# Attention gates as 48 extra columns behind the query projection's token tiles

## The chip, the cores and the metric

The kernel runs on one core of a Trainium2 chip. The metric is the device time of one execution in microseconds, a median of several runs. The engines are named as in the profile: PE is TensorE (matmuls), PEld its loads of the stationary operand, DVE is VectorE, ACT is ScalarE, POOL is GpSimd, SP is SyncE, which only issues transfers.

## The reference, cut to what matters

The program is a decoder trunk of two layers for 512 tokens of width 1024 in float32. Layer 0 has a gated convolution as its mixer, layer 1 a sparse attention with three branches (compressed, selected, windowed); each mixer stands between two half-step SwiGLU networks. The change touches one thing in the attention: the gates that weigh the three branches of the 16 heads.

```python
q, kc, vc, ks, vs, kw, vw, gl = jnp.split(h @ w_in, offs, axis=-1)
gates = jax.nn.sigmoid(gl.astype(f32)).reshape(bsz, seq, G, Hg, 3).transpose(0, 2, 3, 1, 4)
...
out = gb[..., 0:1] * o_c + gb[..., 1:2] * o_s + gb[..., 2:3] * o_w
```

`gl` are the last 48 columns of the attention's input projection (16 heads x 3 branches); `h` is the normalized input, 512 x 1024. For each token, head and branch one number in 0 to 1 results.

## The kernel before, in words

**Precision.** A float32 product is made of three fp32r matmuls: each operand is split into a high part and a low remainder (`split`, lines 175 to 177: ACT copies the high part, DVE subtracts), and the products high-high, high-low and low-high are summed in PSUM (`mm3`, lines 184 to 187). A matmul has a stationary operand, loaded first (PEld), and a moving operand, whose columns stream past it. In the profile a matmul is written out<-moving,stationary.

**Activations** lie transposed: `h` is 8 tiles of 128 features x 512 tokens, each with a high and a low part (`h[0][k]`, `h[1][k]`; hhi and hlo in the profile).

**Two kinds of projection.** `project` (line 204) holds a weight tile of 128 x 128 and streams 512 tokens past it; its result has features on the partitions. `natural` (line 737) holds a tile of 128 tokens x 128 features of `h` and streams 256 columns of weights past it; its result has tokens on the partitions, which queries, keys and values need. `natural(c, each)` loads its weights at once, in two parts of 4 x 128 rows (`nsa_in`, line 711), and returns two jobs, each for half of the tokens: a PSUM tile `nat`, two token tiles, 8 steps of k each, three matmuls a step, so 48 matmuls; then `each` takes the result out of PSUM.

**The gates** (line 946) use `project`: the 48 columns, padded to 128 with zeros, are the stationary operand, so that 24 matmuls of 512 columns give 48 x 512 in PSUM (`gl`). ACT takes the exponential of the negative, four transposes on TensorE turn it to tokens on partitions (`pg`), DVE adds 1 and takes the reciprocal into `gsb`. The attention reads `gsb` (lines 1048 and 1103).

**Where this stands.** `nsa` (line 715) first makes four projections with `head_start` (`hs`), then the preparation in `es2` (lines 829 to 862): the compressor of keys and values in steps (`c0`, `c1`; its copies `t` out of `hs`, its split blocks `flh` and `fll`, its matmuls `ph`), the query projection of group 0 (`q0`, projection 0), the key projections 8 and 6, the gates, and the value projection 7. Then `attend` runs 32 units, with the remaining projections spread among them in steps.

**Buffers and order.** Weights come through a shared pool of three buffers each for the raw, high and low part (`wraw`, `whi`, `wlo`; line 189); a weight is transferred by SP's queue as soon as a raw buffer is free and split as soon as its other two are. Projections 8, 6 and 7 take their second part from a pool of their own (`nw`). PSUM has eight banks: two for each of the tags nat, s, t and o; a tile named mm takes the first three in turn (`six`, line 75). The program is written without an explicit order among engines: the tile framework puts each engine's instructions in order when the program is built, by a planner that simulates when each is ready and otherwise prefers the one earlier in the program, and sets the semaphores. Each engine then runs its list in order.

## Time and profile before

| | |
|---|---|
| median of 3 runs | 1948.66 us (1947.72 to 1952.35) |
| the profiled execution's own time | 1950.15 us |
| its span, first to last instruction | 1948.4 us |
| granted TensorE clock | 1.00 |
| PE busy / DVE busy / ACT busy | 98% / 75% / 45% |
| head_start of the attention ends, query projection begins | 1280.0 us |
| gates' projection | 1327.5 to 1333.0 us |
| gates' transposes | 1341.2 to 1341.5 us |

How to read it: an instruction has a start and a duration from the span's start; a matmul's duration includes a latency that overlaps the next matmul, so the pace of a stream is read from the starts. Groups show busy time, the mean of one, and the idle time of the engine ahead of them with what ended it. A row of a stretch shows its length and then the busy time of PE, PEld, DVE, ACT and POOL with the number of instructions, the granted clock, the share of the DMA engines and GB/s.

### The profile page before, as it was taken

The numbers are of one execution on the slowest core, as the hardware profiler recorded it, in microseconds if no ns is written. First come the engines' busy times: TensorE is split into PE (matmuls) and PEld (weight loads), VectorE is DVE, ScalarE is ACT, GpSimd is POOL, SyncE is SP. The second block draws the span as 40 slices with busy tenths as digits, with TensorE's granted clock in tenths as the row PEclk, the third lists the DMA queues.
The fourth block names the chain that finished last, engine by engine and source line by source line (L and its number), as shares of the span: only waits on it lengthen the run. The fifth ranks groups of instructions, "written<-read, shape, count | busy, mean of one in ns | idle before, by whom it ended". The sixth has DMA issues, their size and how long they took to land.

```text
span 1948.4 us, 32290 instructions
## 1 busy us (share of the span) xinstructions
PE 1905.9 (98%) x12600; PEld 1727.0 (89%) x12600; DVE 1458.0 (75%) x2519; ACT 869.3 (45%) x1401; POOL 194.4 (10%) x294
## 2 busy tenths in 40 slices
PE   6999999999999999999999999999999899999999
PEld 4888888898899898999989899999888789898989
DVE  7888888674467586868868686885787987685965
ACT  4322222342235353434635343465887865353532
POOL 0000000100010000000000000002444420000000
PEclk9999999999999999999999999999999999999999
DMA  8889889522145664634566463235433433665621
GB/s 313 310 318 329 311 323 326 202 98 98 65 122 160 158 173 125 168 104 120 154 165 174 125 167 103 78 127 144 112 69 66 115 82 115 186 163 143 174 82 65
DMA packets 113670, 313.42 MB, mean 161 GB/s; under 512 B 13995, under 2 KB 14267, under 8 KB 113516
## 3 DMA queue, kind: packets, MB, share of 16 engines
q1 hardware_dynamic: 96208, 273.88, 41.4%
q0 software_dynamic: 17216, 37.33, 11.1%
q8 instruction: 99, 1.62, 0.3%
q14 instruction: 55, 0.45, 0.1%
q10 hardware_dynamic: 92, 0.14, 0.0%
HBM read 308.15 MB, written 3.15 MB: 160 GB/s over the span
## 4 chain that ended last, share of the span: by engine, by line
PE 86%; DVE 5%; ACT 4%; DMA 2%; issue 2%; SPq 1%; POOL 0%; DVEq 0%; ACTq 0%; POOLq 0%
PE gu L186 13%; PE gu L185 13%; PE gu L187 13%; PE y L186 7%; PE y L185 7%; PE y L187 7%; PE hs L186 2%; PE hs L187 2%; PE hs L185 2%; PE cv L186 2%; PE cv L185 2%; PE cv L187 2%; PE ty L186 2%; PE ty L185 2%; PE ty L187 2%
## 5 line engine op out<-in xcount | busy, mean ns | idle before, releaser
L176 ACT ACTIVATE whi<-wraw 128x1024 fp32r<-128x1024 f32 (+2 forms) x274 | 270.8, 996 | 494.5 <-PE y L186 203.8
L177 DVE TENSOR_TENSOR wlo<-wraw,whi 128x1024 fp32r<-128x1024 f32 (+2 forms) x274 | 311.3, 1141 | 59.4 <-ACT whi L176 57.4
L186 PE MATMUL gu<-hlo,whi 128*128 128x256 f32 (+1 forms) x880 | 278.2, 316 | 0.0
L185 PE MATMUL gu<-hhi,whi 128*128 128x256 f32 (+1 forms) x880 | 278.1, 316 | 0.0
L187 PE MATMUL gu<-hhi,wlo 128*128 128x256 f32 (+1 forms) x880 | 277.4, 315 | 0.0
L186 PE MATMUL y<-alo,whi 128*128 128x512 f32 x587 | 229.2, 390 | 0.2 <-DVE alo L177 0.2
L185 PE MATMUL y<-ahi,whi 128*128 128x512 f32 x587 | 229.1, 390 | 0.0
L187 PE MATMUL y<-ahi,wlo 128*128 128x512 f32 x587 | 228.9, 390 | 0.0
L131 DVE CUSTOM_DVE_ANT_0 adaraw<-adaraw,cond 128x1024 f32<-128x1024 f32 x144 | 174.5, 1222 | 41.8 <-DMA adaraw<-in_adaw 39.2
L185 PEld LDWEIGHTS gu<-hhi,whi 128*128 128x128 f32 x880 | 165.2, 188 | 12.9
L187 PEld LDWEIGHTS gu<-hhi,wlo 128*128 128x128 f32 x880 | 165.2, 188 | 12.3
L186 PEld LDWEIGHTS gu<-hlo,whi 128*128 128x128 f32 x880 | 165.2, 188 | 12.0
L523 POOL DMA_DIRECT2D qa<-in_ffi x54 | 65.0, 1204 | 794.5 <-DMA qa<-in_ffi 261.8
L185 PEld LDWEIGHTS y<-ahi,whi 128*128 128x128 f32 x587 | 110.2, 188 | 23.6 <-ACT ahi L176 0.4
L186 PEld LDWEIGHTS y<-alo,whi 128*128 128x128 f32 x587 | 110.2, 188 | 23.6 <-DVE alo L177 0.5
L187 PEld LDWEIGHTS y<-ahi,wlo 128*128 128x128 f32 x587 | 110.2, 188 | 23.3
L599 DVE SCALAR_TENSOR_TENSOR x<-y,mods,x 128x512 f32<-128x512 f32 x72 | 53.4, 750 | 93.7 <-PE y L187 93.6
L185 PE MATMUL gu<-th,qbh 128*128 128x256 f32 x432 | 119.6, 277 | 2.2 <-ACT qbh L176 2.2
L187 PE MATMUL gu<-th,qbl 128*128 128x256 f32 x432 | 119.6, 277 | 0.7 <-DVE qbl L177 0.7
L186 PE MATMUL gu<-tl,qbh 128*128 128x256 f32 x432 | 119.3, 276 | 0.0
L185 PE MATMUL gu<-th,qah 128*128 128x256 f32 x432 | 119.2, 276 | 0.0
L186 PE MATMUL gu<-tl,qah 128*128 128x256 f32 x432 | 119.2, 276 | 0.0
(314 smaller groups left out, 5059.9 us busy)
## 6 DMA issues: line engine op xcount, KB each, us to landing
adaraw<-in_adaw SPq DMA_DIRECT2D x144, 512.0 KB, 6.2
wraw<-in_ffi SPq DMA_DIRECT2D x122, 512.0 KB, 4.1
qa<-in_ffi SPq DMA_DIRECT2D x108, 256.0 KB, 4.0
qa<-in_ffi POOLq DMA_DIRECT2D x54, 512.0 KB, 6.8
wraw<-in_ffo SPq DMA_DIRECT2D x72, 384.0 KB, 4.2
a<-in_ffi SPq DMA_DIRECT2D x54, 256.0 KB, 4.1
wraw<-in_cwi SPq DMA_DIRECT2D x24, 512.0 KB, 3.3
wraw<-in_nwi SPq DMA_DIRECT2D x20, 512.0 KB, 3.9
```

The source lines that it names most:

```text
L131: nc.vector.tensor_tensor_reduce(out=raw, in0=raw, in1=cond, scale=1.0, scalar=0.0, op0=ALU.mult, op1=ALU.add, accum_out=m)
L176: nc.scalar.activation(hi, src, AF.Copy)
L177: nc.vector.tensor_tensor(lo, src, hi, ALU.subtract)
L185: nc.tensor.matmul(o, sh, mh, start=first, stop=False)
L186: nc.tensor.matmul(o, sh, ml, start=False, stop=False)
L187: nc.tensor.matmul(o, sl, mh, start=False, stop=last)
L523: nc.gpsimd.dma_start(qa, bass.AP(tensor=a21.tensor, offset=a21.offset, ap=[a21.ap[0], [0, 2], a21.ap[1]]), accum_op=ALU.add)
L599: lambda d, o: nc.vector.scalar_tensor_tensor(x[d], o, mod(s, 2, d), x[d], op0=ALU.mult, op1=ALU.add))
```

## The change

The gates lose their own projection. The query projection of group 0 gets a second PSUM tile (`gl`) and the gate weights as a third weight tile. In each step of k, while it goes through the token tiles, it streams the first 48 columns of the gate weights' high and low part past the same token tile as the query weights: two matmuls of 48 columns ahead of the two with hhi, one ahead of the one with hlo. The result has tokens on the partitions at once, 4 x 48 columns in one PSUM bank; the four transposes go, and Exp, addition and reciprocal follow at the end of the query projection's second half, on 128 partitions x 192 columns. The gate weights are allocated, transferred and split together with the query projection's. Without a gate, the matmuls of `natural` and their order are those of before.

```diff
-            def natural(c, each, own=None):
+            def natural(c, each, own=None, gate=None):
                 w = nsa_in(c, own)
+                if gate:
+                    gw, go = weights(nwg, KD, P), psum("gl")
...
                         for k in range(KD):
-                            wh, wl = w[k // 4]
-                            mm3(oc, h[0][k][:, tk], h[1][k][:, tk], wh[:, k % 4, :], wl[:, k % 4, :],
-                                k == 0, k == KD - 1)
+                            wh, wl = [p[:, k % 4, :] for p in w[k // 4]]
+                            hh, hl = [p[k][:, tk] for p in h]
+                            first, last = k == 0, k == KD - 1
+                            if gate:
+                                gc = slice((2 * hf + t) * 48, (2 * hf + t + 1) * 48)
+                                gh, gl = [p[:, k, 0:48] for p in gw]
+                                nc.tensor.matmul(go[:, gc], hh, gh, start=first, stop=False)
+                                nc.tensor.matmul(go[:, gc], hh, gl, start=False, stop=False)
+                            nc.tensor.matmul(oc, hh, wh, start=first, stop=False)
+                            nc.tensor.matmul(oc, hh, wl, start=False, stop=False)
+                            if gate:
+                                nc.tensor.matmul(go[:, gc], hl, gh, start=False, stop=last)
+                            nc.tensor.matmul(oc, hl, wh, start=False, stop=last)
                     each(hf, o)
+                    if gate and hf:
+                        gate(go)
...
-                q0 = natural(0, raw(query_tiles(0), vq))
+                q0 = natural(0, raw(query_tiles(0), vq), gate=partial(gates, gsb))
...
-                g = gates(es2, h, gsb)
-                next(g)
...
-                next(g, None)
...
-    def gates(es, h, gsb):
-            o = psum("gl")
-            w = weights(nwg, KD, P)
-            project(o, w, 0, h, [(k, k) for k in range(KD)], True, True)
-            e = tmp("gle")[0:48]
-            nc.scalar.activation(e, o[0:48], AF.Exp, scale=-1.0)
-            yield
-            pg = psum("pg", "o")
-            for t in range(NB):
-                nc.tensor.transpose(pg[:, t * 48:(t + 1) * 48], e[:, t * P:(t + 1) * P], ident[0:48, 0:48])
-            ge = tmp("ge", NB * 48)
-            nc.vector.tensor_scalar(ge, pg[:, 0:NB * 48], 1.0, None, op0=ALU.add)
-            nc.vector.reciprocal(gsb.rearrange("p a b -> p (a b)"), ge)
+    def gates(gsb, o):
+        n = NB * 48
+        e = tmp("gle", n)
+        nc.scalar.activation(e, o[:, 0:n], AF.Exp, scale=-1.0)
+        nc.vector.tensor_scalar(e, e, 1.0, None, op0=ALU.add)
+        nc.vector.reciprocal(gsb.rearrange("p a b -> p (a b)"), e)
```

## The prediction

> **What bounds the kernel now.** I read the page's totals first, then the chain of waits.

> ```profile
> span 1948.4 us, 32290 instructions
> PE 1905.9 (98%) x12600; PEld 1727.0 (89%) x12600; DVE 1458.0 (75%) x2519; ACT 869.3 (45%) x1401; POOL 194.4 (10%) x294
> ...
> PE 86%; DVE 5%; ACT 4%; DMA 2%; issue 2%; SPq 1%; POOL 0%; DVEq 0%; ACTq 0%; POOLq 0%
> ```

> TensorE is busy 98% of the span, and 86% of the chain that ended last is its matmuls. The average says nothing about the stage that is edited, so next I read the busy time by stretches of the attention layer's preparation and of the attention behind it (length, then busy time of each engine).

> ```profile
> 1280.00:1291.30 11.30, 11.30 (x98) 11.30 (x97) 10.82 (x13) 8.66 (x12) 0.00 (x0) 1.00 0.52 174
> 1291.30:1303.00 11.70, 11.70 (x103) 11.70 (x102) 9.55 (x19) 5.42 (x9) 0.00 (x0) 1.00 0.38 128
> 1303.00:1315.00 12.00, 11.59 (x98) 11.15 (x97) 11.83 (x23) 9.08 (x12) 0.00 (x0) 1.00 0.50 156
> 1315.00:1327.40 12.40, 12.28 (x104) 12.04 (x103) 11.83 (x30) 5.87 (x10) 0.00 (x0) 1.00 0.36 115
> 1327.40:1333.00 5.60, 5.60 (x27) 4.58 (x26) 5.16 (x13) 3.49 (x4) 0.79 (x1) 1.00 0.71 220
> 1333.00:1345.00 12.00, 12.00 (x104) 11.74 (x103) 5.44 (x11) 7.07 (x11) 2.18 (x4) 1.00 0.86 201
> ...
> 1363.00:1400.00 37.00, 34.50 (x252) 30.64 (x251) 27.34 (x90) 30.17 (x77) 18.14 (x36) 1.00 0.54 133
> 1400.00:1600.00 200.00, 186.89 (x1263) 164.58 (x1262) 169.50 (x471) 156.87 (x378) 83.24 (x167) 1.00 0.36 83
> ```

> From 1280 to 1345 us TensorE stands still for 0.41 + 0.12 us in all, at a granted clock of 1.00. DVE is its near rival only from 1303 to 1327 (11.83 of 12.00). So whatever TensorE is given or spared here goes almost whole into the time. In the attention, from 1363 us on, it idles 2.50 + 13.11 us.

> **What is removed.** The gates' own projection and its four transposes, in order of time, each with the first instruction behind it:

> ```profile
> 1327.52 0.39 PE L185 MATMUL gl<-hhi,whi 128*128 128x512 f32 x1
> ...
> 1333.02 0.27 PE L938 MATMUL pk<-ident,kd 128*128 128x128 f32 x1
> ...
> 1341.15 0.44 PE L955 MATMUL pg<-ident,gle 48*128 48x48 f32 x4
> 1341.53 0.39 PE L185 MATMUL nat<-whi,hhi 128*128 128x256 f32 x1
> ```

> The 24 matmuls of 512 columns take 1333.02 - 1327.52 = 5.50 us (229 ns each; the 0.39 is a latency that overlaps the next one). The transposes take 1341.53 - 1341.15 = 0.38 us. Nothing else could have run on TensorE in either place. Removed: 5.88 us.

> **What is added.** The query projection of group 0 gets 4 token tiles x 8 k x 3 = 96 matmuls of 48 moving columns. Their stationary operand is the token tile, 128x128, which a neighbouring projection matmul uses too. Does the second use of a tile load it again? In the kernel before, the first two matmuls of each triple already share it (hhi), and the groups of loads say:

> ```profile
> L185 PEld LDWEIGHTS nat<-whi,hhi 128*128 128x128 f32 x256 | 48.4, 189 | 0.6 <-ACT kq L1029 0.5
> L186 PEld LDWEIGHTS nat<-wlo,hhi 128*128 128x128 f32 x256 | 48.3, 189 | 0.3 <-DVE wlo L177 0.3
> ```

> 256 loads for each: every matmul loads its own stationary operand, shared or not. So the edit adds 96 loads of 128 columns, and the question is their pace behind matmuls too short to hide them. The trace has such places: four matmuls of 1 column (L271), and an fp32r matmul of 128 columns in the attention (loads in order of time):

> ```profile
> 1259.00 0.53 PEld L271 LDWEIGHTS pr<-ones,nacc 128*128 128x128 f32 x4
> 1259.44 0.19 PEld L187 LDWEIGHTS hs<-hhi,wlo 128*128 128x128 f32 x1
> ...
> 1394.53 0.19 PEld L1133 LDWEIGHTS o<-ptl,vn 128*128 128x128 f32 x1
> 1394.64 0.66 PEld L1076 LDWEIGHTS s<-k,q 128*128 128x128 f32 x4
> ```

> (1259.44 - 1259.00) / 4 = 110 ns, and 1394.64 - 1394.53 = 110 ns again. For comparison the pace of the 256-column matmuls of this projection, 48 of them in its first half, and the slowest stream of columns in the trace:

> ```profile
> 1280.02 0.28 PE L185 MATMUL nat<-whi,hhi 128*128 128x256 f32 x1
> ...
> 1285.68 0.28 PE L185 MATMUL nat<-whi,hhi 128*128 128x256 f32 x1
> ...
> 4.40 7.16 PE L699 MATMUL pt<-oh,rbn 33*128 33x512 f32 x8 [4.40 <-DMA oh<-in_onehot]
> ```

> That is 5.66 / 48 = 118 ns for 256 columns, so 0.46 ns a column and 22 ns for 48. Even at the plain f32 rate of L699, 7.16 / 8 / 512 = 1.75 ns a column, 48 columns take 84 ns, less than the load. The load sets the price however the columns stream. Bounds for one added matmul: 22 ns below (if the shared load fell away) and 118 ns above (the pace of its neighbours); I take 112, close to the 110 of the load rows. 96 x 0.112 = 10.8 us, bounds 2.1 and 11.3.

> [...]

> **What is moved.** The gate weights' transfer, their split, the Exp with its table load, and the addition and reciprocal:

> ```profile
> 1250.61 3.44 SPq L196 DMA_DIRECT2D wraw<-in_nwi  x2
> ...
> 1278.49 1.32 ACT L888 ACTIVATE t<-hs 64x256 f32<-64x256 f32 x2 [0.69 <-DVE t L886]
> 1279.60 1.07 ACT L176 ACTIVATE whi<-wraw 128x1024 fp32r<-128x1024 f32 x1
> ...
> 1280.70 1.23 DVE L177 TENSOR_TENSOR wlo<-wraw,whi 128x1024 fp32r<-128x1024 f32 x1 [0.23 <-ACT whi L176]
> ...
> 1334.12 1.28 ACT L951 ACT_TABLE_LOAD   x1
> 1335.41 0.59 ACT L951 ACTIVATE gle<-gl 48x512 f32<-48x512 f32 x1
> ...
> 1341.71 0.34 DVE L957 TENSOR_SCALAR ge<-pg 128x192 f32<-128x192 f32 x1
> 1342.09 1.35 DVE L958 RECIPROCAL gsb<-ge 128x192 f32<-128x192 f32 x1
> ```

> The order of allocation makes the gate weights third in the shared ring of three weight buffers, in the place that keys' projection 8 has now: its transfer is the second of the two issued by 1254 us on SP's queue, long before its use, and its split is the ACT and DVE pair at 1279.60 and 1280.70. The gate's low half is needed by the second matmul of the query projection, at 1280.14. If the split stays where that pair is, it ends at 1281.93 and TensorE waits 1.8 us. But ACT was idle 0.69 us ahead of 1278.49, and the split now stands ahead of the copies `t` in the program, so it can begin near 1278.2, when the first weights' buffer comes free, and end near 1280.6. I take 0.6 us, bounds 0 and 1.8. Queued behind it are the copies `t` on ACT and DVE, which only the compressor waits for; the projection's longer stay (11.3 + 10.8 us) hides them.

> Projection 8 then has to take the first buffer that the query projection gives back, 12 of its matmuls and 12 gate matmuls before its end (12 x 0.118 + 12 x 0.112 = 2.8 us), and its split takes 1.07 + 1.23 = 2.3 us. It just fits while ACT and DVE are free: 0.2 us, bounds 0 and 1.8 (one operation of 1.2 us ahead of it on each engine). Exp, table load, addition and reciprocal, 3.6 us in two engines, fall into a stretch with ACT busy 5.42 of 11.70 and DVE 9.55; nothing reads the gates before the attention: 0. If that cover were gone they would cost their 3.6 us. Against this, DVE gets the longer query projection to run ahead in, and the 0.53 us of TensorE's stalls up to 1327 may go: -0.3, bounds -0.5 and 0.

> **The sum.** -5.9 + 10.8 + 0.6 + 0.2 - 0.3 = +5.4 us. The profiled execution took 1950.15 us (span 1948.4 and 1.75 around it), so 1955.6 by its own measure; it lies 1.5 us above the median, 1948.66, and against that the forecast is 1954.1 us, 0.28% slower.

> **The rivals.** The first ends on the other side: *the shared tile is held*, and an added matmul costs only its stream. Then 96 x 22 ns = 2.1 us, minus 5.9: -3.8, 1944.9 us. It decides from a mean price under 5.88 / 96 = 61 ns. For it speaks only that two neighbours share the tile; against it the 256 loads of the second matmul of a triple. Chance 0.05.

> *The gate weights come late*: both waits at their upper bound, 10.8 - 5.9 + 1.8 + 1.8 = +8.5, 1957.2 us. For it speaks that all three buffers are held to the query projection's end, against it that ACT and DVE have little else there. Chance 0.16.

> *The removed projection was a cover.* Behind it runs projection 7, whose weights came just in time:

> ```profile
> 1328.65 1.06 ACT L176 ACTIVATE whi<-wraw 128x1024 fp32r<-128x1024 f32 x1 [2.80 <-DMA wraw<-in_nwi]
> ...
> 1329.75 1.23 DVE L177 TENSOR_TENSOR wlo<-wraw,whi 128x1024 fp32r<-128x1024 f32 x1
> ```

> They end at 1330.98; with 5.5 us less ahead of it the projection would want them near 1328.1 and wait 2.9 us: +8.3, 1957.0 us. Against it: the gate weights leave the ring of transfers and buffers at the same place, so each later weight moves up by one. Chance 0.06.

> *The attention's order turns out otherwise.* Its instructions are put in order by a planner from their simulated readiness, and buffers rotate one step differently. TensorE idles 15.6 us there; a third of it, 5.2 us, gained or lost, gives 1948.9 or 1959.3 us. Nothing in the profile speaks for a sign: 0.14 for a gain (0.05 of it large enough to pass below the bound), 0.07 for a loss.

> **How the numbers follow.** A measurement of this kernel tells about 0.3% (5.8 us) from no change, so from 1942.8 to 1954.5 it is the same. The forecast has 0.52: with its small terms from 0 to 1 us, 0.37 of it lies within the bound and 0.15 above. Slower by over 0.3%: 0.15 + 0.16 + 0.06 + 0.07 = 0.44. Within: 0.37 + 0.05 + 0.09 = 0.51. Faster: 0.05. The range of 8 in 10 runs from 1947, which leaves out the held tile and a large gain, to 1959, which takes in both late weights and their bound on the load's pace.

> **What would show it.** Right: 96 more loads on TensorE in the query projection, its two halves lasting 11.3 + 10.8 us, added matmuls 110 to 118 ns apart, no gl matmuls of 512 columns, one table load still between the first and the last. Wrong: loads fewer than matmuls or a pace under 61 ns (the held tile); over 1 us of TensorE's idle at the query projection's first matmuls or at projection 8's, released by a low half (late weights); a wait at projection 7 (the cover); TensorE's idle from the attention's start to its end more than 3 us from 15.6.

## The result, and the profile after

The changed kernel takes 1956.53 us, the median of 18 runs (1953.89 to 1979.27); the kernel before takes 1949.11 us, also over 18 runs (1946.53 to 1952.35). The ratio is 1.0051, with a 95% interval of 1.0036 to 1.0066: slower, and by more than the 0.28% of the forecast, whose size of 5.4 us against the new 1949.11 would have been 1954.5 us. The medians lie 7.4 us or 0.38% apart; the means, 1958.96 and 1949.05 us, have the ratio 1.0051, because two of the 18 runs lie far above the others (1972.49 and 1979.27). The profiled execution took 1960.1 us. First its page (totals, then the line of the chain of waits that gives shares by engine):

```profile
span 1958.3 us, 32424 instructions
PE 1913.9 (98%) x12668; PEld 1736.5 (89%) x12668; DVE 1458.8 (74%) x2519; ACT 869.6 (44%) x1401; POOL 193.9 (10%) x294
...
PE 86%; DVE 6%; ACT 4%; DMA 2%; issue 2%; SPq 0%; POOL 0%; DVEq 0%; ACTq 0%; POOLq 0%
```

There are 12668 - 12600 = 68 matmuls more, and as many loads: 96 came, 24 + 4 went, and none of the 96 shares the load of its neighbour. Next the busy time of the kernel after by stretches, from the last of the head start to the end of the attention's own matmuls (length, then PE, PEld, DVE, ACT, POOL, the granted clock, the transfers). The borders are here the first matmuls of each part: query projection, projection 8, compressor's matmuls mixed with projection 6, projection 7 and the turning of keys and queries, attention.

```profile
1281.17:1304.23 23.06, 22.41 (x195) 22.21 (x194) 14.38 (x16) 10.56 (x14) 0.00 (x0) 1.00 0.30 104
1304.23:1315.54 11.31, 11.31 (x98) 11.31 (x97) 7.82 (x18) 5.36 (x8) 0.00 (x0) 1.00 0.47 141
1315.54:1340.58 25.04, 24.62 (x205) 23.91 (x203) 24.30 (x53) 15.92 (x22) 0.00 (x0) 1.00 0.41 135
1340.58:1364.92 24.34, 24.34 (x213) 24.23 (x212) 9.90 (x24) 11.88 (x21) 7.92 (x17) 1.00 0.73 170
1364.92:1586.70 221.78, 206.21 (x1375) 179.43 (x1373) 184.84 (x532) 184.53 (x450) 101.05 (x203) 1.00 0.38 89
```

The query projection lasts 23.06 us instead of 11.28 (1280.02 to 1291.30 before): +11.78. From its first matmul to the first attention logit (1364.92) it is 83.75 us; the same stretch of before is 78.24 us. So the edited stage costs +5.5 us. The attention took 221.78 us against 221.94. The rows of the kernel before for its last two parts, beside the last two above:

```profile
1333.02:1358.27 25.25, 25.25 (x217) 25.01 (x216) 7.78 (x15) 12.33 (x20) 7.09 (x17) 1.00 0.63 140
1358.27:1580.21 221.94, 206.36 (x1375) 179.39 (x1373) 185.12 (x532) 184.32 (x450) 100.91 (x203) 1.00 0.38 88
```

Where the extra matmuls stand is seen in the order of time on PE, with the idle time in brackets:

```profile
1281.17 0.29 PE L754 MATMUL gl<-whi,hhi 128*128 128x48 f32 x1
...
1281.50 0.28 PE L757 MATMUL nat<-wlo,hhi 128*128 128x256 f32 x1
1282.42 0.29 PE L755 MATMUL gl<-wlo,hhi 128*128 128x48 f32 x1 [0.65 <-DVE wlo L177]
...
1282.87 0.19 PE L754 MATMUL gl<-whi,hhi 128*128 128x48 f32 x1
...
1283.56 0.19 PE L754 MATMUL gl<-whi,hhi 128*128 128x48 f32 x1
...
1340.46 0.28 PE L187 MATMUL ph<-whi,fll 128*128 128x256 f32 x1
1340.58 0.27 PE L949 MATMUL pk<-ident,kd 128*128 128x128 f32 x1
```

One step of k, with three narrow and three wide matmuls, lasts 1283.56 - 1282.87 = 0.69 us; three wide ones lasted 0.354, so a narrow one costs 0.112 us. The first matmul with the gate weights' low half waits for it, although the planner has put two wide matmuls ahead of it. And the last two rows show the other side of the change: the compressor's last matmul is followed at once by the transpose that before stood behind the 24 matmuls of the gates.

The remaining difference of this profile lies outside the edited stage. Of the 9.9 us by which the two spans differ, 1.2 lie ahead of the stage, 5.5 in it, -0.2 in the attention and 3.4 behind it. The mean clock is 0.997: in two places, from 629.1 for 3.4 us and from 1612.2 for 6.8 us, TensorE ran at half its clock. Together that is 10.2 us at half clock, worth at most 5.1 us. The kernel before has the second place too, in another execution of it (below).

### The profile page after: what moved, and what is told of

Same layout as the page of the kernel before. It is cut to its first block, busy times and chain, and to the rows that moved or that the text cites. A ratio compares the mean times of both kernels' runs of the same rounds, so it can differ in the third digit from the quotient of the medians.

```text
span 1958.3 us, 32424 instructions
## 1 busy us (share of the span) xinstructions
PE 1913.9 (98%) x12668; PEld 1736.5 (89%) x12668; DVE 1458.8 (74%) x2519; ACT 869.6 (44%) x1401; POOL 193.9 (10%) x294
## 4 chain that ended last, share of the span: by engine, by line
PE 86%; DVE 6%; ACT 4%; DMA 2%; issue 2%; SPq 0%; POOL 0%; DVEq 0%; ACTq 0%; POOLq 0%
PE gu L186 13%; PE gu L187 13%; PE gu L185 13%; PE y L186 7%; PE y L185 7%; PE y L187 7%; PE hs L186 2%; PE hs L187 2%; PE hs L185 2%; PE cv L186 2%; PE cv L185 2%; PE cv L187 2%; PE ty L186 2%; PE ty L185 2%; PE ty L187 2%
## 5 line engine op out<-in xcount | busy, mean ns | idle before, releaser
L176 ACT ACTIVATE whi<-wraw 128x1024 fp32r<-128x1024 f32 (+2 forms) x274 | 271.2, 997 | 500.5 <-PE y L186 213.7
L177 DVE TENSOR_TENSOR wlo<-wraw,whi 128x1024 fp32r<-128x1024 f32 (+2 forms) x274 | 312.9, 1147 | 66.7 <-ACT whi L176 64.8
L186 PE MATMUL gu<-hlo,whi 128*128 128x256 f32 (+1 forms) x880 | 278.2, 316 | 0.0
L185 PE MATMUL gu<-hhi,whi 128*128 128x256 f32 (+1 forms) x880 | 278.0, 316 | 0.0
L187 PE MATMUL gu<-hhi,wlo 128*128 128x256 f32 (+1 forms) x880 | 277.4, 315 | 0.0
L186 PE MATMUL y<-alo,whi 128*128 128x512 f32 x587 | 229.2, 390 | 0.1
L185 PE MATMUL y<-ahi,whi 128*128 128x512 f32 x587 | 229.0, 390 | 0.0
L187 PE MATMUL y<-ahi,wlo 128*128 128x512 f32 x587 | 228.9, 390 | 0.0
L185 PEld LDWEIGHTS gu<-hhi,whi 128*128 128x128 f32 x880 | 165.2, 188 | 12.9
L187 PEld LDWEIGHTS gu<-hhi,wlo 128*128 128x128 f32 x880 | 165.2, 188 | 12.3
L186 PEld LDWEIGHTS gu<-hlo,whi 128*128 128x128 f32 x880 | 165.2, 188 | 12.0
L186 PEld LDWEIGHTS y<-alo,whi 128*128 128x128 f32 x587 | 110.2, 188 | 23.5 <-DVE alo L177 0.5
L187 PEld LDWEIGHTS y<-ahi,wlo 128*128 128x128 f32 x587 | 110.2, 188 | 23.4
L185 PEld LDWEIGHTS y<-ahi,whi 128*128 128x128 f32 x587 | 110.2, 188 | 23.2
L185 PE MATMUL gu<-th,qbh 128*128 128x256 f32 x432 | 120.3, 278 | 2.4 <-ACT qbh L176 2.4
L187 PE MATMUL gu<-th,qbl 128*128 128x256 f32 x432 | 120.3, 279 | 0.7 <-DVE qbl L177 0.7
L186 PE MATMUL gu<-tl,qbh 128*128 128x256 f32 x432 | 120.1, 278 | 0.0
L185 PE MATMUL gu<-th,qah 128*128 128x256 f32 x432 | 119.2, 276 | 0.0
L186 PE MATMUL gu<-tl,qah 128*128 128x256 f32 x432 | 119.2, 276 | 0.0
```

What stands on the lines that cost most here:

```text
L176: nc.scalar.activation(hi, src, AF.Copy)
L177: nc.vector.tensor_tensor(lo, src, hi, ALU.subtract)
L185: nc.tensor.matmul(o, sh, mh, start=first, stop=False)
L186: nc.tensor.matmul(o, sh, ml, start=False, stop=False)
L187: nc.tensor.matmul(o, sl, mh, start=False, stop=last)
```

## The experiments

The table puts all runs side by side. "Stage" is the time from the query projection's first matmul to the first attention logit, from each trace; "half clock" names the stretches inside that stage in which the records show a granted clock of 0.5.

| kernel | stage us | half clock in the stage us | median us (runs) | ratio, 95% interval |
|---|---|---|---|---|
| before | 78.24 | none | 1949.11 (18) | |
| before, again | 78.26 | none | 1948.2 (11) | 1.0002, 0.9994 to 1.0011 |
| after | 83.75 | none | 1956.53 (18) | 1.0051, 1.0036 to 1.0066 |
| after, again | 83.70 | none | 1955.61 (5) | 1.0033, 1.0020 to 1.0046 |
| wide128 | 84.15 | none | 1954.93 (5) | 1.0033, 1.0021 to 1.0045 |
| gate_first | 83.09 | none | 1953.7 (9) | 1.0025, 1.0015 to 1.0035 |
| moved | 78.62 | none | 1949.12 (11) | 1.0005, 0.9996 to 1.0013 |
| joined | 77.65 | none | 1948.17 (11) | 1.0000, 0.9992 to 1.0009 |
| joined_nw | 76.47 | none | 1946.73 (12) | 0.9994, 0.9986 to 1.0003 |
| late_narrow | 89.46 | 13.7 | 1962.95 (6) | 1.0069, 1.0056 to 1.0082 |
| double | 121.63 | 58.0 | 1991.03 (6) | 1.0155, 1.0103 to 1.0207 |
| forced_before | 91.00 | 3.4 and 6.8 | 1963.8 (4) | 1.0078, 1.0065 to 1.0091 |
| forced_after | 95.02 | 23.9 | 1969.43 (4) | 1.0108, 1.0095 to 1.0122 |
| forced_wide | 93.52 | 17.1 | 1965.22 (4) | 1.0087, 1.0073 to 1.0102 |

The last three and joined_nw were timed against 1948.35 us of before (17 runs), the others of their batches against 1949.06 (14) or 1948.74 (29). The ratio of double is that of four of its six runs, without the two longest, and not that of its median.

### The price of a narrow matmul: again, wide128, gate_first

The kernel after once more, as a measure for the two beside it:

> The changed kernel once more, unaltered, for the spread of its times and of the granted clock. Theory A (the path sum: 96 loads of 110 to 113 ns and a 0.9 us wait, less 5.9 us, make about 5.3 us; what lies above it comes from short stretches at half clock that fall on any kernel by chance): runs with a granted clock of 1.000 lie 5 to 6 us above the kernel before, and the clock goes below 0.995 no more often than in the kernel before. Theory B (the change itself makes the clock drop: the wait and the sparse columns in the query projection): some runs of 15 have a clock below 0.995 and times 10 to 30 us above the rest, the kernel before has none.

wide128 streams all 128 padded columns of the gate weights, 80 of them zeros, in place of 48:

```diff
-                                gc = slice((2 * hf + t) * 48, (2 * hf + t + 1) * 48)
-                                gh, gl = [p[:, k, 0:48] for p in gw]
+                                gc = slice((2 * hf + t) * P, (2 * hf + t + 1) * P)
+                                gh, gl = [p[:, k, :] for p in gw]
...
-        nc.scalar.activation(e, o[:, 0:n], AF.Exp, scale=-1.0)
+        nc.scalar.activation(e.rearrange("p (a b) -> p a b", b=48), o.rearrange("p (a b) -> p a b", b=P)[:, :, 0:48], AF.Exp, scale=-1.0)
```

> The 96 gate matmuls stream 128 columns (48 and 80 zero columns of the padded weights) where they streamed 48; the same number of loads. Theory A (the load sets the price): 128 columns take 57 ns, under the load's 110, so the time is that of the changed kernel within 1 us and the query projection lasts 22 to 23.5 us. Rival (the stream sets the price, as a fixed cost and so much a column): 96 x 80 x 0.44 ns = 3.4 us more. Theory B (sparse columns let the clock drop): the same time at clock 1.000, but fewer runs below 0.995 than the changed kernel.

gate_first has the gate weights allocated ahead of the query weights:

```diff
-                w = nsa_in(c, own)
                 if gate:
                     gw, go = weights(nwg, KD, P), psum("gl")
+                w = nsa_in(c, own)
```

> The gate weights are allocated ahead of the query projection's own, so that the last of the three buffers to come free goes to the query weights' second part, which is needed four steps of k later. Theory A: the wait of 0.9 us at the first gate matmul with the low half goes, and nothing takes its place: 0.9 us less than the changed kernel, 4.4 us above the kernel before at clock 1.000. Rival: the wait moves to the second part of the query weights, no gain. Theory B (the wait is what makes the clock drop): no run below 0.995.

wide128 has 2.7 times the columns, the same ratio as the repeated kernel after, and a stage 0.4 us longer. On PE, in order of time, the first matmuls of three steps of k:

```profile
1289.99 0.22 PE L754 MATMUL gl<-whi,hhi 128*128 128x128 f32 x1
...
1290.67 0.22 PE L754 MATMUL gl<-whi,hhi 128*128 128x128 f32 x1
...
1291.36 0.22 PE L754 MATMUL gl<-whi,hhi 128*128 128x128 f32 x1
```

What costs is not the columns: 48 or 128 of them come at the same pace of 0.69 us a step. It is what each matmul brings along, and every one here brings a load, whose pace in the prediction's rows is 110 ns. Another fixed cost of a matmul of about that size can't be told from the load by these runs, since no matmul here comes without one. In gate_first the wait at the start is gone (no wait of PE's in the query projection), the stage is 0.6 us shorter (0.9 was expected), and the ratio falls by 0.08 points, which the intervals can't tell from nothing. The wait was real and small; the price of the 96 matmuls is the bulk.

### The place or the form: moved, joined, joined_nw

moved keeps the projection of 24 matmuls of 512 columns and its four transposes and only puts them where the change puts its columns, between the halves of the query projection:

```diff
+                g = gates(es2, h, gsb)
...
-                run(q0)
+                run(q0[:1])
+                next(g)
+                run(q0[1:])
+                next(g, None)
...
-                g = gates(es2, h, gsb)
-                next(g)
...
-                next(g, None)
```

> The kernel before with its own form of the gates (24 matmuls of 512 columns, exponential, four transposes) at the place of the change: between the two halves of the query projection, the gate weights allocated behind the query weights. Only the place differs. Theory A (the place costs next to nothing, the form costs 4.8 us): within 1 us of the kernel before. Rival (the place costs the 0.9 us wait and more behind it, or the cover is missed before projection 7): 1 to 3 us above it.

joined, again an edit of the kernel before, drops the gates' projection and appends the 48 columns to the 256 of the query weights in memory, so that one matmul of 304 columns does both and no load is added. The weights come in three parts of 3, 3 and 2 steps of k, and each token tile has a PSUM tile of its own:

```diff
+            def queries(v):
+                n = CW + 48
...
+                w = [weights(nwq[p][:, 0:m], m, n) for p, m in ((0, 3), (1, 3), (2, 2))]
...
+                            mm3(o[:, 0:n], h[0][k][:, tk], h[1][k][:, tk], wh[:, k % 3, :], wl[:, k % 3, :],
...
-                q0 = natural(0, raw(query_tiles(0), vq))
+                q0 = queries(vq)
...
-                g = gates(es2, h, gsb)
-                next(g)
```

> The 48 gate columns are laid behind the 256 query columns of group 0, so that one matmul streams 304 columns and no load is added; weights in three parts of 3, 3 and 2 steps of k, one PSUM bank for each token tile. Theory A: the load is hidden behind 304 columns (135 ns), so the gates cost 96 x 48 x 0.443 = 2.0 us of streaming; against 5.88 us removed -3.8 us: 1945.2 us, 0.2% under the kernel before, the query projection 13.3 us long; no wait at its start, since the buffer that comes free last holds steps 6 and 7. Rival (the four more PSUM banks or the parts of weights make a wait): -3.8 us plus the wait, between 1945 and 1949. [...]

moved can't be told from before: the place is worth 0.4 us of the stage, so the rest of the 5.5 us is the form's. joined streams its 304 columns in 0.14 us (rows in order of time on PE):

```profile
1279.34 0.30 PE L185 MATMUL nat<-whi,hhi 128*128 128x304 f32 x1
1279.48 0.30 PE L186 MATMUL nat<-wlo,hhi 128*128 128x304 f32 x1
```

Yet its stage is only 0.6 us shorter than before. The waits of PE in joined from 1279 to 1357 us say why (line waited for: total, times, longest):

```profile
PE nat L186 <- DVE wlo L177: 1.8, 2, 1.3
PE po L950 <- DVE hT L945: 0.8, 1, 0.8
PE ph L186 <- DVE wlo L177: 0.4, 1, 0.4
PE pq L974 <- DVE cz L930: 0.4, 1, 0.4
```

Without the gates' projection and transposes (-5.9 us) and with 96 x (0.14 - 0.118) = 2.1 us for the columns the stage would be 3.8 us shorter; but projection 8 waits 1.3 us for its low half, because the third part of the weights holds the third buffer, and the chain on DVE that feeds the compressor's second product and the queries' transposes comes late by 0.8 and 0.4 us. Neither of these two waits is there in before, so the 5.5 us of the removed projection probably covered them; no run tests that by itself. joined_nw takes the first wait away; there the third part comes from the pool of the key projections' second halves.

```diff
-                w = [weights(nwq[p][:, 0:m], m, n) for p, m in ((0, 3), (1, 3), (2, 2))]
+                w = [weights(nwq[p][:, 0:m], m, n, own, 2 if own else 3, wp) for p, m, own in ((0, 3, None), (1, 3, None), (2, 2, nw))]
```

> The joined kernel (48 gate columns appended to the 256 of the query projection, one matmul of 304) with the third part of its weights in the pool that the key projections use for their second halves, so that the ring of three buffers is free for projection 8. Path theory: projection 8's wait for its low half (1.30 us) goes, the query projection waits at most 0.5 us for its third part, whose memory is freed only at its start: 0.8 to 1.3 us less than joined, ratio to before 0.9993 to 0.9996, from query projection to first attention logit 76.4 to 76.9 us (joined 77.65, before 78.25). Rival: the third part comes late by its split (1.06 us on ScalarE and 1.2 on VectorE behind the compression's copies): a wait of 1 to 2 us inside the query projection, the time as joined or slower.

```profile
PE po L950 <- DVE hT L945: 1.1, 1, 1.1
PE nat L186 <- DVE wlo L177: 0.6, 1, 0.6
PE pq L974 <- DVE cz L930: 0.4, 1, 0.4
PE ph L186 <- DVE wlo L177: 0.4, 1, 0.4
```

In joined_nw, by the same view, PE's waits for the low half `wlo` in the projections are down from 1.8 to 0.6 us: that of projection 8 is gone, and 0.6 us are left in a later one. The stage falls to 76.47 us, 1.8 below before and inside the expected 76.4 to 76.9. The whole run, 0.9994, still can't be told from before. So the same idea without the added matmuls is no loss, and with its buffers in order perhaps a gain of a tenth of a per cent.

### What else the narrow columns do: late_narrow, double

late_narrow gives the gates the form of the change (96 matmuls of 48 columns, the token tile stationary), but by themselves, in the old place behind the compressor:

```diff
-                q0 = natural(0, raw(query_tiles(0), vq), gate=partial(gates, gsb))
+                q0 = natural(0, raw(query_tiles(0), vq))
...
+                go, (gh, gl) = psum("gl"), weights(nwg, KD, P)
+                for t in range(NB):
+                    gc = slice(t * 48, (t + 1) * 48)
+                    for k in range(KD):
+                        mm3(go[:, gc], h[0][k][:, t * P:(t + 1) * P], h[1][k][:, t * P:(t + 1) * P],
+                            gh[:, k, 0:48], gl[:, k, 0:48], k == 0, k == KD - 1)
+                gates(gsb, go)
```

> The 96 gate matmuls of 48 columns leave the query projection and run by themselves at the place of the kernel before, between the head turns and projection 7; the result has tokens on the partitions, so there are no transposes. Only the form differs from the kernel before, not the place. Theory A: 96 x 0.111 - 5.88 = +4.8 us against the kernel before, and no wait at the query projection. Rival (the place costs: three buffers held, ring of buffers moved): close to the kernel before, under +2 us. [...]

double streams the 48 columns twice in each step and halves the exponential's scale, so that the same gates come out:

```diff
-                                nc.tensor.matmul(go[:, gc], hh, gh, start=first, stop=False)
-                                nc.tensor.matmul(go[:, gc], hh, gl, start=False, stop=False)
+                                for r in range(2):
+                                    nc.tensor.matmul(go[:, gc], hh, gh, start=first and not r, stop=False)
+                                    nc.tensor.matmul(go[:, gc], hh, gl, start=False, stop=False)
...
-                                nc.tensor.matmul(go[:, gc], hl, gh, start=False, stop=last)
+                                for r in range(2):
+                                    nc.tensor.matmul(go[:, gc], hl, gh, start=False, stop=last and r == 1)
...
-        nc.scalar.activation(e, o[:, 0:n], AF.Exp, scale=-1.0)
+        nc.scalar.activation(e, o[:, 0:n], AF.Exp, scale=-0.5)
```

> The changed kernel with each of the 96 gate matmuls issued twice into the same columns (the sum is halved again in the exponential, so the gates are the same). Theory A, price: 96 more loads of 110 to 113 ns, so 10.6 to 10.9 us more in the query projection than in the changed kernel, whose stage lasts 22.8 to 23.1 us; about 1966.4 us at clock 1.000. [...]

Both are slower than 96 or 192 times 0.112 us explain. Below, a window is a stretch of a trace cut 3.41 us long, like the shortest stretch at half clock (that from 629.1 in the kernel after), with a border where the clock changes. The windows of late_narrow (PE's busy time with the number of matmuls, the granted clock, the transfers):

```profile
1324.26:1327.67 3.41, 3.41 (x32) 1.00 0.66 220
1327.67:1331.09 3.42, 3.42 (x33) 1.00 0.64 199
1331.09:1334.50 3.41, 3.41 (x18) 0.50 0.94 244
...
1341.33:1344.74 3.41, 3.41 (x17) 0.50 0.10 14
1344.74:1348.15 3.41, 3.41 (x31) 1.00 0.94 155
```

TensorE is busy all the time, 3.42 of 3.42 us, and yet its clock is halved from 1331.09 on, after one window of nothing but narrow matmuls; it comes back at 1344.74, at the end of the window in which the wide matmuls begin again. The 96 matmuls take 15.6 us (1325.92 to 1341.56) instead of 96 x 0.112 = 10.8. In double the same happens to the whole query projection:

```profile
1278.55:1281.97 3.42, 2.88 (x26) 1.00 0.96 359
1281.97:1285.38 3.41, 3.41 (x19) 0.50 0.43 161
...
1336.58:1339.99 3.41, 3.41 (x17) 0.50 0.00 0
1339.99:1343.41 3.42, 3.42 (x31) 1.00 0.37 123
```

That is 58.0 us at half clock, from 1281.97 to 1339.99. But double does not always run so: of its six executions four took 1990.9 to 1993.8 us at a mean clock of 0.984 to 0.985, one 1967.1 at 0.997, and one 1962.3 us at 1.000. So the same program kept the full clock in one run and, by its mean clock, lost 1.5 to 1.6% of it in four; the trace is of one of these four.

### Held once halved: forced_before, forced_after, forced_wide

To see what decides whether the clock is held at half, fourteen ScalarE copies out of PSUM, later overwritten, were put ahead of the query projection's first half, in before, after and wide128:

```diff
                     o = psum("nat")
+                    if c == 0 and hf == 0:
+                        for _ in range(14):
+                            nc.scalar.activation(o, os[3], AF.Copy)
```

> The kernel before with fourteen ScalarE copies (128x512, out of PSUM, of a projection that is done) put ahead of the query projection's first matmul, so that TensorE stands idle for some 8 us there; the copies' result is overwritten, nothing of the computation changes. [...] Theory (the sparse columns, not the idle spot alone, keep the clock at half): the idle spot may halve the clock, but it is back within one or two windows of 3.4 us, so the projection takes 11.3 us plus at most 3.4 (half of 6.8). Time: before's 1948.7 plus 6 to 13, with little spread. Rival (an idle spot is enough, what is streamed after it does not matter): the same number here as in the two kernels beside it.

> The kernel after with the same fourteen ScalarE copies ahead of the query projection's first wide matmul; nothing of the computation changes. [...] Rival (the idle spot alone decides): the clock is back within two windows, the projection takes 23 to 27 us, the time is forced_before's plus 5 to 8, 1960 to 1969.

> [...] Rival (the idle spot alone decides): as forced_after.

The planner didn't let TensorE stand idle ahead of the projection. It put other matmuls into the gap, others in each kernel: in forced_before more of the query projection and of projection 8, until a wait of 2.3 us for a low half; in forced_after first a run of gate matmuls by themselves. So the three don't share one idle spot, as was meant. By the times the expected numbers missed: forced_before lies 15.5 us above before, beyond its 6 to 13, and forced_after 5.6 us above forced_before, in the rival's range, and forced_wide 1.4 us above it, under that range. Only the windows can tell the mechanisms apart. First forced_before, then forced_after:

```profile
1286.90:1290.31 3.41, 1.11 (x7) 1.00 0.02 10
1290.31:1293.72 3.41, 3.41 (x19) 0.50 0.44 154
1293.72:1297.14 3.42, 3.42 (x31) 1.00 0.02 5
```

```profile
1276.60:1280.01 3.41, 2.76 (x24) 1.00 0.90 275
1280.01:1283.42 3.41, 3.41 (x33) 1.00 0.88 327
1283.42:1286.84 3.42, 3.42 (x18) 0.50 0.05 22
...
1303.90:1307.32 3.42, 3.42 (x18) 0.50 0.00 0
1307.32:1310.73 3.41, 3.41 (x31) 1.00 0.45 153
```

With wide matmuls behind the idle spot the clock is back after one window, 3.4 us. In forced_after there is no idle spot in the window ahead of the fall (3.41 of 3.41 us busy, all narrow), and with the change's mix of narrow and wide matmuls behind it the clock stays at half for seven windows, 23.9 us, until projection 8 streams only wide ones. All four runs of it have a mean clock of 0.991 or 0.992. In forced_wide, with 128 columns in place of 48, five windows (17.1 us) are held, one of them with a wait of 2.8 us in it. So the rival, that an idle spot alone decides, falls by the window ahead of forced_after's fall, as it does by late_narrow, and not by the times.

What tells these windows apart is what is streamed in them. Three windows of the kernel after, from the end of the head start into the query projection:

```profile
1277.65:1281.06 3.41, 3.41 (x33) 1.00 0.70 214
1281.06:1284.48 3.42, 2.77 (x24) 1.00 0.87 302
1284.48:1287.89 3.41, 3.41 (x32) 1.00 0.66 243
```

The first has 33 matmuls of 256 columns and TensorE busy for 3.41 of 3.41 us, and the clock stays. late_narrow's window from 1327.67 and forced_after's from 1280.01 have 33 each too and are as busy, with 48 columns a matmul, and behind both the clock is halved. TensorE's busy time doesn't order the windows that also hold a wait either: the second one above, with 2.77 us busy in 24 matmuls, kept the full clock behind it, and double's from 1278.55, with 2.88 us in 26, did not. And once halved, the change's mix stayed at half until wide matmuls came by themselves (23.9 us in forced_after, 58.0 in double), where forced_before's wide ones were back after 3.4 us.

Counted from the records of the kernel after (a matmul's columns go to the window in which it starts), its stage puts 3088 columns into the window from 1281.06 and 4560 into the next, where 256-column matmuls put 7424 to 7680 (from 1304.95 and from 1277.65). Its clock stayed at full there all the same. Counted the same way, the two windows of late_narrow and forced_after that a fall followed have 1440 each. At what count a fall would come, and whether it is the columns that the clock follows, these runs don't show.

### The clock windows that aren't the change's: before_again

> The kernel before once more, for a second profile of it: how long the stretches of its span are from run to run. Expected: the stretch from the query projection's first matmul to the attention's first logits 78.2 us as in the first profile, within 0.3; the stretch ahead of it 1 to 2 us shorter than in the first profile (it was 1280.0 us there, and 1277.9 to 1279.1 in three profiles of kernels that are the same up to that point); single stretches of 3.4 us at half clock after idle times of TensorE around 627 and 1610 us, in some profiles and not in others.

The kernel before, profiled a second time, has the same stage (78.26 us), begins its query projection 1.5 us earlier, as expected, and has a halved place at the attention's end, where the kernel after had one from 1612.2:

```profile
1601.59:1605.00 3.41, 1.54 (x11) 1.00 0.01 2
1605.00:1608.41 3.41, 3.41 (x18) 0.51 0.46 156
1608.41:1611.83 3.42, 3.42 (x18) 0.50 0.00 0
```

TensorE waits there 1.1 to 1.2 and 0.7 us for the two parts of `h` in both kernels, in their first profiles as well. In the first profile of before the clock stays at 1.00 there; in that of after it falls for 6.8 us, here as well. The wait is the same, so it alone doesn't decide the fall; what else does is not shown. Such windows cost single runs some microseconds in either kernel and say nothing about the change.

## Why the prediction was right or wrong, point by point

**The path was right, its sum closer than its terms.** The sum was +5.4 us; the stage measured +5.5 in two traces of the kernel after (83.75 and 83.70 against 78.24). Part by part, with the rows above: query projection +11.8, projection 8 +0.1, compressor and projection 6 none, gates' projection -5.5, the rest up to the attention -0.9.

- *Added, 96 x 0.112 = 10.8 us*: 0.112 us a matmul. That the columns don't set the price is shown by wide128; that it is the load and no other fixed cost rests on the equal pace of the load rows. The rival of the held tile falls: 68 more matmuls, 68 more loads, and a step of 0.69 us.
- *Removed, 5.88 us*: the compressor's last matmul and the next transpose follow at once, and nothing took the room. Behind it 0.5 us more went than the transposes' 0.38: half of projection 7's matmuls start every 0.113 us and not every 0.118. That gain has no term in the sum.
- *The start's wait, 0.6*: it is 0.8, the 0.92 us from 1281.50 to 1282.42 less the usual 0.11. The split of the gate weights did not begin as early as forecast, 1.8 us ahead of the projection (1278.2 against 1280.02), but 1.1 us ahead of it (1280.05 against 1281.17), behind two of the copies `t` (ACT of the kernel after, in order of time):

```profile
1278.28 0.64 ACT L899 ACTIVATE t<-hs 64x256 f32<-64x256 f32 x1 [1.16 <-PE hs L187]
1279.61 0.65 ACT L899 ACTIVATE t<-hs 64x256 f32<-64x256 f32 x1 [0.69 <-DVE t L897]
1280.05 1.07 ACT L176 ACTIVATE whi<-wraw 128x1024 fp32r<-128x1024 f32 x1
```

- *Projection 8's wait, 0.2*: did not come; projection 8 lasts 11.31 us, all of it busy. The rival of the late gate weights held at the start by less than half of its 1.8 and here not at all.
- *Recovered stalls, -0.3*: did not come. The stretch of the compressor's matmuls lasts 25.04 us, as before, with 0.42 us idle.
- *Exp, table, reciprocal, 0*: right; the attention begins without a wait. *The removed cover*: no wait at projection 7 here. In joined and joined_nw, where less stands ahead, there is a wait of 0.8 to 1.1 us at the compressor's second product.
- *The attention's order*: 221.78 against 221.94 us. Nothing there.

That the sum came within 0.1 us is luck: the errors of its terms (start +0.2, pace of the added matmuls +0.2, stalls +0.3, projection 8 -0.2, pace of projection 7 -0.5) cancel.

**The outcome was not.** The likeliest case was "within 0.3%", and the change is slower by 0.51%, interval 0.36 to 0.66; the path's 5.5 us alone are 0.28%. So the step that failed is the one by which the path's sum is the whole change of the time: "at a granted clock of 1.00. [...] So whatever TensorE is given or spared here goes almost whole into the time." The clock was read as given and got no term, and with a sum 0.02 points under the bound any cost outside the path decides the case. What the runs show in its place: the means lie 9.9 us apart, and of that the path is 5.5, the two far runs, with mean clocks of 0.989 and 0.986, are 2.1 (without them the mean is 1956.84), and 2.3 us stay open.

The change fills TensorE's time, but not its columns: 4560 in a window in place of 7424, and only 3088 in the first one, in which TensorE also waits for the gate weights. The traced run stayed at full clock through the stage. That another run can lose it there and then be held at half is the author's estimate, from forced_after, whose same mix was held for 23.9 us. Two of the 18 runs of the kernel after, 1972.49 and 1979.27 us at mean clocks of 0.989 and 0.986, would fit it: at half clock a matmul of this stage takes 3.41 / 16 = 0.213 us (forced_after's windows: 16 begin in each), 192 of them 41 us, 18 us more than 23. They have no trace, so this cause is inferred, from double and forced_after, and not shown in the kernel after itself; gate_first, without the wait, had no such run in 9, but neither had the repeated kernel after in 5 nor wide128 in 5, so these are too few to show it.

In the repetition the means lie 6.7 us apart, of which 1.2 are not the path's. There the clock of every run of both kernels is on record, and time at half clock (an estimate: the missing share of the clock, as 1 - 0.998, times the span, averaged over the runs) makes 0.7 us of the 1.2. For the 18 runs of before in the first comparison only the profiled one has its clock on record, so the 2.3 us can't be split that way. Nothing in the traces of the edited stage or of the attention answers to that rest, and the starts of the query projection, which vary from 1276.4 to 1281.2 us over the profiles, don't order themselves by the change.

## What to carry to other kernels

Matmuls that share a stationary operand each brought their own load here: columns that ride along are only cheap inside the same matmul (22 ns for 48 more columns in joined, 112 ns for 48 on their own). Where a change puts short matmuls into a stretch, read the granted clock beside the busy time: late_narrow, with TensorE busy 3.42 of 3.42 us, lost half its clock for 13.7 us, and forced_after stayed at half for 23.9 us, until wide matmuls came. And a removed projection is also cover: give the chain that ran behind it its time back before counting the gain (joined waited 0.8 and 0.4 us there).
